# A held first store and two aligned loop heads in a masked softmax kernel

## The chip, the cores and the metric

The kernel runs on one core of one Trainium2 chip. The metric is the device time of one execution in microseconds (us); lower is better. The kernel before takes 156.9 us (median of four runs, 156.85 to 157.22). The granted clock was 1.0 in every run.

## The reference, cut to what matters

```python
batch, heads, seq_q, seq_k = 16, 8, 256, 256
x = randn(batch, heads, seq_q, seq_k)                  # float32, 33.6 MB
lengths = randint(seq_k // 2, seq_k, size=batch)       # one length for each batch entry
result = zeros_like(x)
for b in range(batch):
    n = lengths[b]
    e = exp(x[b, :, :, :n] - max(x[b, :, :, :n], axis=-1))
    result[b, :, :, :n] = e / sum(e, axis=-1)
```

Each batch entry is one *tile* of 2 MB: 128 partitions, 16 rows on each, 256 columns. The input is read once and the output written once. Columns beyond the length must come out as zero.

## The kernel before

Tiles 0 to 3 are loaded by SyncE, tiles 4 to 15 by GpSimd, which reads the tile's length and loads only about as many columns as are needed. VectorE masks a tile, ScalarE takes exponentials with row sums, VectorE divides, SyncE stores. There are eight tile slots in SBUF.

```python
# SyncE: five loads (tile 0 in halves), then all stores, on one queue
for h in range(2):
    nc.sync.dma_start(out=xt[:, 0, s], in_=x_f[0, :, s]).then_inc(s_ld[h], 16)
for b in range(1, ahead):                                    # ahead = 4
    nc.sync.dma_start(out=xt[:, b], in_=x_f[b]).then_inc(s_ld[b + 1], 16)
for b in range(batch):
    for s in parts(b):                                       # whole, halves or quarters of a tile
        nc.sync.wait_ge(s_out, ...)                          # VectorE has divided it
        nc.sync.dma_start(out=out_f[b, :, s, :], in_=xt[:, b % slots, s, :]).then_inc(...)
# GpSimd: waits, then a loop of 6 turns with two tiles each
nc.gpsimd.wait_ge(s_word, 16)                                # lengths are in SBUF
nc.gpsimd.wait_ge(s_fill, slots - ahead)                     # zeros are in slots 4 to 7
nc.gpsimd.wait_ge(s_ld[ahead - 1], 16)                       # tile 2 has landed
with nc.Fori(0, (batch - ahead) // 2, 1, engines=[POOL]) as q:
    for par in range(2):
        ...                                                  # read the length, wait for the slot
        pick(...)                                            # nested If/Else: one of 12 widths, one load
# ScalarE: a loop of 32 turns, half a tile each
with nc.Fori(0, 2 * batch, 1, engines=[ACT]) as i:
    nc.scalar.wait_ge(s_min, i + 1)
    ...                                                      # 8 activations, the last one increments s_exp
```

The softmax here doesn't subtract the row's maximum and nothing guards it: scores larger than these inputs give would overflow.

## Time and profile before

| What | Before | Where it is read |
|---|---|---|
| median of the runs | 156.9 us | timed runs |
| span of the profiled run | 155.3 us | page, first line |
| bytes moved, mean rate | 62.06 MB, 400 GB/s | page, HBM line |
| busiest engine | VectorE, 74% | page, busy totals |
| first store issued by SyncE | 18.86 us | timeline |
| first load issued by GpSimd | 20.94 us | timeline |
| instruction queue q14 | 2 packets | DMA queues |

The DMA engines limit this kernel: the DMA row is at 9 in 38 of 40 slices, and no compute engine is busier than 74%. So a profile of it is read by asking in which stretch the DMA engines move less than they can, not which compute engine is busy. The lines are in the prediction.

### The profile page before, as it was taken

The numbers are of one execution on the slowest core, as the hardware profiler recorded it, in microseconds if no ns is written. First come the engines' busy times: TensorE is split into PE (matmuls) and PEld (weight loads), VectorE is DVE, ScalarE is ACT, GpSimd is POOL, SyncE is SP. The second block draws the span as 40 slices with busy tenths as digits, with TensorE's granted clock in tenths as the row PEclk, the third lists the DMA queues.
The fourth block names the chain that finished last, engine by engine and source line by source line (L and its number), as shares of the span: only waits on it lengthen the run. The fifth ranks groups of instructions, "written<-read, shape, count | busy, mean of one in ns | idle before, by whom it ended". The sixth has DMA issues, their size and how long they took to land.

```text
span 155.3 us, 1316 instructions
## 1 busy us (share of the span) xinstructions
PE 0.2 (0%) x1; PEld 0.1 (0%) x1; DVE 115.6 (74%) x84; ACT 105.2 (68%) x514; POOL 19.0 (12%) x25
## 2 busy tenths in 40 slices
PE   0000000000000000000000000000000000000000
PEld 0000000000000000000000000000000000000000
DVE  1249999951999697997969696969698639796600
ACT  3087799992492978869595959596886906959100
POOL 4910031000220020200211020202000000000000
DMA  4999999999999999999999999999999999999991
GB/s 127 426 443 422 443 304 398 419 411 442 412 410 390 415 411 419 406 415 417 402 423 410 414 411 405 417 417 416 413 425 410 423 436 441 414 443 426 420 426 65
DMA packets 9988, 62.08 MB, mean 400 GB/s; under 512 B 850, under 2 KB 946, under 8 KB 6274
## 3 DMA queue, kind: packets, MB, share of 16 engines
q1 hardware_dynamic: 5904, 41.95, 65.7%
q0 software_dynamic: 4080, 20.12, 32.0%
q14 instruction: 2, 0.02, 0.0%
q10 hardware_dynamic: 2, 0.00, 0.0%
HBM read 28.51 MB, written 33.55 MB: 400 GB/s over the span
## 4 chain that ended last, share of the span: by engine, by line
DMA 77%; issue 7%; DVE 3%; ACT 3%; POOLq 3%; SPq 1%; ACTq 0%; POOL 0%; DVEq 0%
DMA xt<-in_x_dram 77%; ACT xt L252 3%; DVE xt L195 2%; DVE xt L222 1%; POOLq L99 1%; POOLq L135 1%; POOLq L130 1%; SPq L109 1%; ACTq L252 0%; POOL xt L130 0%; SPq L111 0%; POOLq L157 0%; DVE inv_sum L219 0%; POOLq L153 0%; POOLq L159 0%
## 5 line engine op out<-in xcount | busy, mean ns | idle before, releaser
L252 ACT ACTIVATE xt<-xt x256 | 102.4, 401 | 37.5 <-DVE xt L195 37.5
L222 DVE TENSOR_TENSOR xt<-xt,inv_sum 128x2048 f32<-128x2048 f32 x32 | 73.4, 2292 | 1.1
L252 ACT ACTIVATION_READ_ACCUMULATOR xt<-xt x256 | 47.8, 187 | 0.0
L195 DVE SCALAR_TENSOR_TENSOR xt<-down,len_s,xt 128x2048 f32<-128x2048 f32 (+1 forms) x17 | 37.8, 2222 | 13.3 <-DMA xt<-in_x_dram 13.2
L130 POOL DMA_DIRECT2D xt<-in_x_dram x12 | 12.8, 1064 | 95.6 <-issue 53.0
L219 DVE RECIPROCAL inv_sum<-row_sum 128x8 f32<-128x8 f32 x32 | 6.4, 199 | 14.4 <-ACT xt L252 14.4
L149 POOL MEMSET xt<- 128x1536 f32 x4 | 5.3, 1386 | 1.3 <-DVE len_s L186 1.3
L244 ACT ACT_TABLE_LOAD x1 | 1.3, 1283 | 1.6 <-SPq L79 1.6
L178 DVE TENSOR_SCALAR down<-iota_i 128x256 f32<-128x256 int32 x1 | 0.3, 298 | 1.6 <-POOL iota_i L141 1.6
L183 DVE CAST len_b<-word 1x16 bf16<-1x16 int32 x1 | 0.2, 161 | 0.5 <-DMA word<-in_lengths_dram 0.5
L186 DVE TENSOR_SCALAR len_s<-len_f 128x16 f32<-128x16 f32 x1 | 0.2, 175 | 0.4 <-PE len_f L165 0.4
L141 POOL IOTA iota_i<- 128x256 int32 x1 | 0.3, 332 | 0.6 <-SPq L79 0.6
L146 POOL MEMSET seed<- 1x1 f32 x2 | 0.3, 162 | 0.0
L244 ACT ACTIVATE warm<-const-float32-0.0 128x1 f32<-128x1 f32 x1 | 0.2, 203 | 0.0
L144 POOL MEMSET ones<- 1x128 bf16 x1 | 0.2, 194 | 0.0
L165 PE MATMUL len_f<-len_b,ones 1*128 1x16 bf16 x1 | 0.2, 168 | 2.8 <-DVE len_b L183 2.8
L270 POOL MEMSET const-float32-0.0<- 128x1 f32 x1 | 0.1, 98 | 0.3 <-issue 0.3
L165 PEld LDWEIGHTS len_f<-len_b,ones 1*128 1x128 bf16 x1 | 0.1, 97 | 2.7 <-POOL ones L144 2.7
L270 POOL MEMSET const-float32-1.0<- 128x1 f32 x1 | 0.1, 98 | 0.0
L270 POOL MEMSET const-bfloat16-1.0<- 128x1 bf16 x1 | 0.1, 98 | 0.0
L270 POOL MEMSET const-uint8-127<- 128x1 uint8 x1 | 0.1, 98 | 0.0
L270 POOL BASE_LOAD x1 | 0.0, 17 | 0.1
## 6 DMA issues: line engine op xcount, KB each, us to landing
out_dram<-xt SPq DMA_DIRECT2D x19, 1024.0 KB
out_dram<-xt SPq DMA_DIRECT2D x14, 512.0 KB
xt<-in_x_dram SPq DMA_DIRECT2D x3, 2048.0 KB, 16.2
out_dram<-xt SPq DMA_DIRECT2D x3, 2048.0 KB
xt<-in_x_dram POOLq DMA_DIRECT2D x3, 1728.0 KB, 17.0
xt<-in_x_dram POOLq DMA_DIRECT2D x2, 2048.0 KB, 18.9
xt<-in_x_dram POOLq DMA_DIRECT2D x2, 1600.0 KB, 17.2
xt<-in_x_dram POOLq DMA_DIRECT2D x2, 1280.0 KB, 14.5
```

The costliest lines, as they stand in the source:

```text
L99: return nc.values_load(at, engines=[engine], skip_runtime_bounds_check_because="compared with constants, never an address",)
L109: nc.sync.dma_start(out=xt[:, 0, s], in_=x_f[0, :, s]).then_inc(s_ld[h], 16)
L130: nc.gpsimd.dma_start(out=xt[:, slot, :, :w], in_=x_n[:, n, :, :w]).then_inc(s_sw[par], 16)
L135: with nc.gpsimd.If(v <= ws[m]):
L149: nc.gpsimd.memset(xt[:, b, :, low:], 0.0).then_inc(s_fill, 1)
L165: nc.tensor.matmul(len_f, lhsT=ones, rhs=len_b, start=True, stop=True).then_inc(s_lenf, 1)
L195: return nc.vector.scalar_tensor_tensor(out=t, in0=down[:, None, lo:hi].to_broadcast([P, s.stop - s.start, hi - lo]), scalar=len_s[:, b : ...
L219: step(nc.vector.reciprocal(out=inv_sum[:, b, s], in_=row_sum[:, b, s]))
L222: nc.vector.tensor_tensor(out=t, in0=t, in1=inv_sum[:, b, s, None].to_broadcast([P, half, seq_k]), op=ALU.mult,).then_inc(s_out, 1)
L244: nc.scalar.activation(out=warm, in_=nc.const_aps.tensor(0.0, (P, 1), F32), func=EXP)
L252: ins = nc.scalar.activation(out=e, in_=e, func=EXP, accum_out=sum_h[:, bass.ds(i, 1), j])
L270: nc = _bacc.Bacc("TRN2", target_bir_lowering=False, num_devices=1)
```

## The change

The intent, as far as the diff tells it: SyncE's first store is held a little, out of the way of the last loads, and the two loops that run from registers start at a fixed place of an instruction block. `head_slot` names that place; slot 0 is the head of the block.

```diff
         for b in range(1, ahead):
             nc.sync.dma_start(out=xt[:, b], in_=x_f[b]).then_inc(s_ld[b + 1], 16)
+
+        nc.sync.wait_ge(s_exp, 3)
         for b in range(batch):
...
-        with nc.Fori(0, (batch - ahead) // 2, 1, engines=[POOL]) as q:
+        with nc.Fori(0, (batch - ahead) // 2, 1, engines=[POOL], head_slot={POOL: 0}) as q:
...
-        with nc.Fori(0, 2 * batch, 1, engines=[ACT]) as i:
+        with nc.Fori(0, 2 * batch, 1, engines=[ACT], head_slot={ACT: 0}) as i:
```

## The prediction

> **What bounds the kernel now.** I read the page first: the busy totals, then the two DMA rows over 40 slices.
>
> ```profile
> PE 0.2 (0%) x1; PEld 0.1 (0%) x1; DVE 115.6 (74%) x84; ACT 105.2 (68%) x514; POOL 19.0 (12%) x25
> ...
> DMA  4999999999999999999999999999999999999991
> GB/s 127 426 443 422 443 304 398 419 411 442 412 410 390 415 411 419 406 415 417 402 423 410 414 411 405 417 417 416 413 425 410 423 436 441 414 443 426 420 426 65
> ...
> HBM read 28.51 MB, written 33.55 MB: 400 GB/s over the span
> ```
>
> No compute engine is above 74%, while the DMA row is at 9 in every slice but the first and the last. So the span is the time to move 62.06 MB plus the two ends at which nothing moves. One slice is 155.3/40 = 3.88 us. Only one inner slice stands out, the sixth (19.4 to 23.3 us): its engines are as busy as the others and yet it moves 304 GB/s.
>
> Second I cut the span into stretches. The columns are the stretch, its length, busy time of the five engines, the TensorE clock, the DMA share and GB/s.
>
> ```profile
> 5.00:20.30 15.30, 0.00 (x0) 0.00 (x0) 11.14 (x8) 10.15 (x51) 3.52 (x3) 1.00 1.02 434
> 20.30:23.30 3.00, 0.00 (x0) 0.00 (x0) 2.97 (x3) 3.00 (x16) 1.30 (x1) 1.00 0.99 284
> 23.30:36.00 12.70, 0.00 (x0) 0.00 (x0) 9.89 (x8) 12.61 (x64) 0.56 (x1) 1.00 0.99 409
> 36.00:134.00 98.00, 0.00 (x0) 0.00 (x0) 79.94 (x57) 69.45 (x343) 10.91 (x10) 1.00 1.02 416
> 134.00:152.00 18.00, 0.00 (x0) 0.00 (x0) 11.02 (x8) 8.49 (x42) 0.00 (x0) 1.00 1.00 425
> 152.00:155.30 3.30, 0.00 (x0) 0.00 (x0) 0.00 (x0) 0.00 (x0) 0.00 (x0) 1.00 0.07 27
> ```
>
> The reader sees 434 GB/s while only loads move, 409 to 416 with loads and stores together, 425 with stores alone, and in between a **dip** of 3.0 us at 284. The share in the dip is still 0.99, so the queues are not empty: the same packets take longer. Against 434 the dip loses 3.0 x (1 - 284/434) = 1.04 us. That is the only loss that this change can reach.
>
> Third, what happens in the dip, from the timeline (start, length) and, the last two lines, the chain of work that ended last:
>
> ```profile
> 18.86 0.42 SPq L118 DMA_DIRECT2D out_dram<-xt  x1
> 18.93 2.35 DVE L195 SCALAR_TENSOR_TENSOR xt<-down,len_s,xt 128x2048 f32<-128x2048 f32 x1
> ...
> 19.45 0.40 ACT L252 ACTIVATE xt<-xt  x1
> 19.76 0.19 ACT L252 ACTIVATION_READ_ACCUMULATOR xt<-xt  x1
> ...
> 20.94 1.30 POOL L130 DMA_DIRECT2D xt<-in_x_dram  x1 [12.42 <-issue]
> ```
>
> ```profile
> 20.95 0.50 POOL xt L130
> 21.48 1.37 POOLq L99
> ```
>
> SyncE issues its first store at 18.86 us, while the last of the five SyncE loads (tile 3) is still moving on the same queue: the DMA view of 20.3 to 23.3 us has 99.4% of its packets' time on q1, the SyncE queue, all but three of its packets full size. GpSimd begins its first own load at 20.94 us. Both stand ahead of the dip, so both are suspects.
>
> [...] Here the first load was issued at 1.13 us and the stretch 1 to 2 us moves nothing, so it is nearer 1.0 us; I use 1.0. [...] In this trace the instruction queue moved 2 packets in all, and the back edges of GpSimd's loop took 52 ns and of ScalarE's 45 ns (medians by source line), so no loop stalls now.
>
> **The change part by part.** *The wait.* It adds one condition to SyncE's first store; the instruction order confirms that only that store gains a semaphore, and no other instruction on SyncE moves. The third increment of that semaphore comes with ScalarE's 24th activation. The eight of tile 1's first half start at 16.64 and end with the accumulator read at 19.76 + 0.19 = 19.95 us. The store would so be issued at about 19.97 us instead of 18.86: 1.1 us later. Does that leave the DMA engines without work? Load 3 ends at 23.2 us at the dip's pace, or at 23.2 - 1.04 = 22.2 without a dip. The store can move from 19.97 + 1.0 = 21.0 us, at least 1.2 us earlier. So it costs nothing directly, and no DMA time is added.
>
> What it may save: if the queued store causes the dip, that begins 20.3 - 18.86 = 1.44 us after the issue, and would now begin at 19.97 + 1.44 = 21.4 us. From 20.3 to 23.3 us the engines did 3.0 - 1.04 = 1.96 us worth of full-rate work. At full rate until 21.4, 1.1 us of it is done, 0.86 us is left; at the dip's rate, 284/434 = 0.65, that takes 1.32 us and loses 0.46. Saving: 1.04 - 0.46 = about **0.6 us**. If the dip has another cause, the saving is zero.
>
> *The loop heads.* Each gets an alignment ahead of its loop: one jump executed once on each engine, some 0.05 us by the 52 ns of the branches here, plus at worst one block fetch. ScalarE reaches its loop at 3.1 us and its first data at 8.2: 5 us of slack hide that. GpSimd reaches its loop at 18.7 us, with nothing hidden there; I put a missed block at 1 to 2 us (an estimate, from the 1.0 us of a first byte here and 0.3 us for 8 KB at one engine's 434/16 GB/s). Its first load moves from 26.3 us on (the GpSimd queue, q0, has no packet in the DMA view before) and would then move at about 27.5. But store 0 alone fills the engines until about 28.3 us (2.1 MB at 409 GB/s after 23.2), with tile 1's stores queued behind it, so they would move stores meanwhile. In the loops nothing is removed, because there is no stall to remove. Cost on the path: zero.
>
> *Is a saving kept until the end?* Stores alone run from 134 us on at 425 GB/s with share 1.00, so the end is backlog, not the last tile's compute. The second-last tile's store is issued at 140.09 and can move at 141.1; but it and the last tile are 4.2 MB, 9.9 us at 425 GB/s, and end at 153.5, so it begins at about 143.6, behind the store ahead of it. So there is 2.5 us of slack, and 0.6 us carries to the end.
>
> Sum: 0 to -0.6 us from the wait, 0 from the loop heads.
>
> **The rivals.** (A) *The queued store slows the load ahead of it.* For: this is the only place where a load and a store share the SyncE queue and the only dip. GpSimd's second length read, at 21.48 us, takes 1.37 us against 0.50 for its first; later ones, beside stores, also take about 1 us[...]. Against: [...]the packets are not slower before 20.3. Result: 156.3 us.
>
> (B) *GpSimd's first transfer causes the dip*[...]. For: the strongest slowing, in the stretches of 21 to 23 us, starts with its DMA instruction at 20.94. Against: its third load, issued at 39.57, has one of 365 GB/s and then 467, so no dip as deep. Result: the dip stays, 156.9 us; if a block fetch delays GpSimd, the dip only moves along.
>
> (C) *The wait starves the engines or the alignment costs.* If load 3 ended by 21 us, or a fetch were far longer than I think, some tenths would be added: 157.2 us. Against: 1.2 us of margin in one case and 2.5 us of queued stores in the other.
>
> (D) *DVE or ScalarE becomes the bound.* Neither gets any work, and both have over a quarter of the span idle; I give it nothing.
>
> **Range and chances.** With 0.5 for A, 0.35 for B and 0.15 for C: 0.5 x 156.3 + 0.35 x 156.9 + 0.15 x 157.2 = 156.6. I lean a little to A, since someone chose that wait for a purpose: 156.5. The three runs before spread by 0.37 us. Range 155.9 to 157.1: A with a whole dip removed (156.89 - 1.04 = 155.85) at the bottom, C at the top. Two per cent is 3.1 us, three times all that the dip holds, so faster or slower by that much needs something not in this profile: 0.02 each.
>
> **What would show it.** The first store at about 20.0 us. Under A the dip starts about 21.4 us, load 3 ends near 22.7, and the sixth slice is well above 304 GB/s. Under B the dip keeps its place after GpSimd's DMA instruction. Loop heads: medians of the loops' branches unchanged; a gap of over 1 us between GpSimd's wait at 18.7 us and its length read would be a block fetch. The prediction is wrong if the time leaves the range, above all if the DMA row falls below 9 inside the span, or if the mixed rate of 416 GB/s changes with the order of the first transfers: each 1% of it over 98 us is 1 us, which I took to stay as it is.

The sum was 0 to -0.6 us: up to 0.6 us from the wait, 0 from the loop heads. The 1.0 us is measured: the first load was issued at 1.13 us and its first packet moved at 2.14.

## More of the kernel before

One more view of before is needed later, SyncE's own waits. Its columns are: who waited for whom, us in total, number of waits, longest wait.

```profile
SPq L117 <- DMA out_dram<-xt: 98.4, 14, 10.3
SPq L118 <- DVE xt L222: 26.9, 8, 15.0
```

SyncE mostly waits for older stores to land (98.4 us), that is, for DMA engines that are behind, and little for VectorE's results (26.9 us). So a finished store mostly lies ready before the DMA engines can take it.

## The result, and the profile after

The changed kernel takes **159.2 us** (median of four runs, 158.70 to 159.66) beside 156.91 for the kernel before. The ratio is **1.0141** (95% interval 1.0107 to 1.0176), 1.4% slower. Ratios here are the mean time of one kernel's runs over that of the other's in the same rounds, so not quite the ratio of the medians. It is well clear of noise and outside the predicted range of 155.9 to 157.1.

The page of the changed kernel, its DMA rows, and then two stretches of the prediction (stretch, length, busy time of five engines, clock, DMA share, GB/s):

```profile
DMA  4999999989999999999999999999999999996994
GB/s 110 436 430 432 432 422 420 412 241 415 436 436 303 375 413 418 408 422 408 408 418 408 421 406 417 412 413 417 418 416 416 421 422 434 420 451 266 403 399 199
...
q14 instruction: 6, 0.05, 0.1%
```

```profile
20.30:23.30 3.00, 0.00 (x0) 0.00 (x0) 2.97 (x3) 3.00 (x17) 0.00 (x0) 1.00 1.02 429
23.30:36.00 12.70, 0.00 (x0) 0.00 (x0) 10.50 (x8) 12.70 (x66) 1.86 (x2) 1.00 0.93 358
```

The dip at 20.3 to 23.3 us is gone: 429 GB/s instead of 284. But three other slices have fallen, to 241, 303 and 266 GB/s, and two of them have a DMA row below 9. Also, the instruction queue moved six packets instead of two. The timeline says what else is new (start, length):

```profile
20.56 7.82 SPq L120 DMA_DIRECT2D out_dram<-xt  x4
```

```profile
30.33 1.30 POOL L132 DMA_DIRECT2D xt<-in_x_dram  x1 [21.94 <-issue]
```

The first store comes at 20.56 us, about as predicted. GpSimd's first load comes at **30.33 us instead of 20.94**, 9.4 us later. Why is read by source line. Line 155 is GpSimd's loop statement and line 139 the Else branch of the nested choice. The columns are engine, operation, count, shortest/median/longest ns, and the first and last start in us.

```profile
L155 POOLq COMPARE_BRANCH  x7: 38/45/50, 19.5 to 121.3; - x7
L155 POOLq FUSED_REGOPS  x6: 78/78/95, 24.7 to 102.4; - x6
```

```profile
L139 POOLq COMPARE_BRANCH  x7: 38/38/38, 30.3 to 110.7; - x7
```

Before, the loop statement was line 153 and the Else branch line 137:

```profile
L153 POOLq FUSED_REGOPS  x6: 78/78/91, 18.9 to 98.2; - x6
```

```profile
L137 POOLq COMPARE_BRANCH  x7: 38/38/38, 20.9 to 105.9; - x7
```

There are seven branches instead of six: the new one is the jump to the loop head, at 19.5 us. The first instruction of the loop starts at 24.7 us, **5.2 us later**; before it started at once, at 18.9. Then the length is read, the width is chosen, the load's last register move is at 26.8 us, and the next instruction, the branch of line 139, is at 30.3: **3.5 us**, where the same pair took 0.7 us before (20.2 to 20.9). One q14 packet lies in each of these two gaps, 8192 bytes at 23.14 us and at 28.39 us, and each took 0.31 us. So in the changed kernel, GpSimd stood still twice for a piece of its own instructions.

SyncE's waits have turned over. Before, it waited mostly for DMA; now it waits mostly for VectorE:

```profile
SPq L120 <- DVE xt L224: 63.3, 21, 13.4
SPq L119 <- DMA out_dram<-xt: 51.3, 11, 7.2
SPq L117 <- DVE xt L224: 15.6, 1, 15.6
```

That is 78.9 us (63.3 + 15.6) instead of 26.9. The supply of finished stores has run out. The stretches with the losses, first before, then after:

```profile
31.00:36.00 5.00, 0.00 (x0) 0.00 (x0) 2.29 (x1) 4.91 (x26) 0.00 (x0) 1.00 1.01 410
36.00:47.00 11.00, 0.00 (x0) 0.00 (x0) 8.46 (x7) 5.96 (x30) 2.31 (x2) 1.00 1.01 422
47.00:53.00 6.00, 0.00 (x0) 0.00 (x0) 5.78 (x4) 2.91 (x16) 0.00 (x0) 1.00 1.03 403
53.00:142.00 89.00, 0.00 (x0) 0.00 (x0) 72.48 (x52) 66.69 (x331) 8.60 (x8) 1.00 1.02 418
142.00:146.00 4.00, 0.00 (x0) 0.00 (x0) 3.31 (x3) 2.37 (x12) 0.00 (x0) 1.00 1.00 430
```

```profile
31.00:36.00 5.00, 0.00 (x0) 0.00 (x0) 2.87 (x3) 5.00 (x27) 1.19 (x2) 1.00 0.85 276
36.00:47.00 11.00, 0.00 (x0) 0.00 (x0) 3.28 (x3) 1.20 (x6) 1.16 (x1) 1.00 1.03 428
47.00:53.00 6.00, 0.00 (x0) 0.00 (x0) 5.93 (x5) 5.78 (x30) 1.15 (x1) 1.00 0.99 320
53.00:142.00 89.00, 0.00 (x0) 0.00 (x0) 73.90 (x52) 64.94 (x320) 8.63 (x8) 1.00 1.02 418
142.00:146.00 4.00, 0.00 (x0) 0.00 (x0) 2.84 (x3) 3.31 (x17) 0.00 (x0) 1.00 0.61 258
```

Losses, each as length x (1 - rate after / rate before): 31 to 36 us 1.6 us, 47 to 53 us 1.2 us, 142 to 146 us 1.6 us. Gain: the dip at 20.3 us, 1.0 us, and a little at 36 to 47. The net is about 3.2 us, and the span grew by 2.4 (155.3 to 157.7). The remaining difference I did not take apart; part of it is the rounding of rates over long stretches.

How the lateness does this can be followed:
- *31 to 36 us.* The stores of tiles 0 and 1 are done, GpSimd's first load has only begun, and the share falls to 0.85: too little is queued.
- *36 to 47 us.* VectorE and ScalarE have nearly nothing to do (3.28 and 1.20 us busy), because tile 4 has not landed.
- *47 to 53 us.* So there is nothing to store, and GpSimd's loads run alone. From 49 to 51.5 us the DMA view has 102.6% of the packets' time on q0 and 297 GB/s; before, it was shared between both queues at 398.
- *142 to 146 us.* The last loads land late too, and the end of the kernel waits for compute of the last tiles instead of emptying a stock of stores. In the chain that ended last VectorE's share is 14%, after 3% before.

### The profile page after: what moved, and what is told of

It reads as the page before. It is cut to its first block, busy times and chain, and to the rows that moved or that the text cites. A ratio compares the mean times of both kernels' runs of the same rounds, so it can differ in the third digit from the quotient of the medians.

```text
span 157.7 us, 1319 instructions
## 1 busy us (share of the span) xinstructions
PE 0.2 (0%) x1; PEld 0.1 (0%) x1; DVE 115.6 (73%) x84; ACT 105.2 (67%) x514; POOL 19.0 (12%) x25
## 4 chain that ended last, share of the span: by engine, by line
DMA 68%; DVE 14%; issue 7%; ACT 4%; POOLq 1%; SPq 1%; ACTq 1%; DVEq 0%
DMA xt<-in_x_dram 62%; DVE xt L224 7%; DVE xt L197 6%; DMA out_dram<-xt 6%; ACT xt L254 4%; ACTq L254 1%; DVE inv_sum L221 1%; POOLq L137 1%; SPq L109 1%; POOLq L132 0%; SPq L111 0%; SPq L120 0%; DVEq L214 0%; POOLq L159 0%; POOLq L161 0%
```

## The experiments

My theory after the result: the jump to GpSimd's loop head costs everything, because its block fetches come while the DMA engines are full, and a late GpSimd starves the stores. The rivals: the held store starves the queues; ScalarE's head costs; the fetch traffic or the alignment itself costs, not the lateness. All kernels gave correct results. Diffs are against the kernel before unless said otherwise; each group of runs has its own runs of the kernel before on the same chip, with medians of 156.56 to 156.76 us. A "fetched block" below is one packet of the instruction queue (8192 bytes each in the changed kernel).

### The parts one by one

**The wait alone** (e1): both `head_slot` arguments removed from the changed kernel.

```diff
+        nc.sync.wait_ge(s_exp, 3)
```

> SyncE's wait alone, both loops as before. Theory (the jump to GpSimd's loop head costs all): no 5 us gap on GpSimd, first GpSimd load at about 21 us, time 156.3 to 157.1, so the wait alone is harmless. Rival (the wait starves the queues): 158 us or more. For the dip: if the queued store made it, it starts 1.1 us later and loses half as much; if GpSimd's first transfer made it, it stays at 20.3 to 23.3 us with about 284 GB/s.

Measured: 156.66 us, ratio 0.9983 (0.9961 to 1.0005). GpSimd's first load is at 20.79 us. In the dip:

```profile
20.30:23.30 3.00, 0.00 (x0) 0.00 (x0) 2.97 (x3) 3.00 (x17) 1.29 (x1) 1.00 0.99 360
```

360 GB/s instead of 284, with GpSimd where it was. The wait is not what costs. The dip follows the store and not GpSimd, as rival A of the prediction had it.

Repeated with five rounds (e15):

> The wait alone, repeated with more rounds. It halved the dip (0.5 us of DMA time). If that is kept until the end: 0.3 to 0.5 us faster, ratio 0.997 to 0.998. If it is lost again later: 0.999 to 1.001.

Measured: 156.24 us against 156.56, ratio 0.9981 (0.9964 to 0.9998). The wait alone is a small gain, 0.2%, just clear of zero. It is the only version here that beats the kernel before.

**Both heads, no wait** (e2), **GpSimd's head alone** (e3), **ScalarE's head alone** (e4): the `head_slot` arguments of the change, both or one at a time.

> Both loop heads aligned, no wait on SyncE. Theory: GpSimd stalls some 8 us as in the changed kernel, time 158.7 to 159.7. Rival (the wait is what costs): 156.9. If both are needed: in between, near 158.

> GpSimd's loop head alone. Theory: the whole loss, 158.5 to 159.5, perhaps some tenths less than with both, because ScalarE's two blocks are not fetched. Rival (ScalarE's head costs): 156.9.

> ScalarE's loop head alone. Theory: its jump stalls some 5 us from 1.8 us on but ends before its first data, so no ScalarE time is lost; [...]156.9 to 157.5. Rival: a good part of the 2.3 us.

| Kernel | Median us | Ratio (95% interval) | First GpSimd load |
|---|---|---|---|
| both heads | 159.85 | 1.0188 (1.0141 to 1.0234) | 30.54 us |
| GpSimd's head | 159.76 | 1.0210 (1.0177 to 1.0243) | 30.63 us |
| ScalarE's head | 156.88 | 1.0020 (0.9987 to 1.0052) | 21.42 us |

GpSimd's head is the loss. (The instruction queue moved six packets with both heads, four with either, two before.) Both kernels with it came out 0.15 to 0.3 us above the range that was expected. The dip at 20.3 us is there in the first two (300 and 281 GB/s), with GpSimd not starting before 30 us; that refutes rival B of the prediction, GpSimd's first transfer as its cause. ScalarE's jump stalls too, but in its slack. In the changed kernel its loop statement reads:

```profile
L249 ACTq COMPARE_BRANCH  x33: 33/45/50, 1.8 to 146.9; - x33
L249 ACTq FUSED_REGOPS  x32: 41/41/47, 6.9 to 144.1; - x32
```

It jumps at 1.8 us and goes on at 6.9, with one q14 packet in between (5.34 us), while its first data come at 7.8.

### Is it the lateness or the fetch?

**GpSimd held, with no loop head aligned** (three kernels, with 3, 5 and 6 for N), and **GpSimd started earlier**:

```diff
         nc.gpsimd.wait_ge(s_ld[ahead - 1], 16)
+        nc.gpsimd.wait_ge(s_exp, N)
```

```diff
-        nc.gpsimd.wait_ge(s_ld[ahead - 1], 16)
+        nc.gpsimd.wait_ge(s_ld[ahead - 2], 16)
```

> The kernel before, no alignment, GpSimd held ahead of its loop until ScalarE's fifth half tile (about 26.3 us), so its first load comes at about 28.5 us without any fetch. Theory (only the lateness counts, not the fetch): a part of the loss, 157.3 to 158.5. Rival (fetch traffic or cold instructions cost): 156.9.

> The same with the sixth half tile: first GpSimd load at about 31.7 us, a little later than the 30.5 us of the aligned kernels. Theory: the whole loss, 159 to 160.5, with stores running out about 32 us, slow stretches near 48 to 52 us and DMA engines idle near 144 us as in the aligned kernels. Rival: 156.9.

> The kernel before with GpSimd held ahead of its loop until ScalarE's third half tile (about 19.95 us), so that its first load comes at about 22.1 us, as in the kernels that reach the loops early. If 1.2 us of lateness makes the rest: 157.4 to 158. By the line through the other held kernels (0.22 us for each us): 156.9. If neither this nor e16 costs, the fetched blocks are left as the cause.

> The kernel before with GpSimd waiting for tile 1 instead of tile 2, so its first load is issued near 16 us instead of 21. If the time goes with GpSimd's start on both sides (0.22 us for each us, from the held kernels), 155.5 to 156.2. If the start before is already early enough to keep both kinds of transfer going: 156.4 to 157.2.

| First GpSimd load | Kernel | Median us | Ratio (95% interval) |
|---|---|---|---|
| 15.74 us | started earlier | 156.92 | 1.0007 (0.9978 to 1.0036) |
| 20.94 us | before | 156.6 to 156.8 | 1 |
| 22.18 us | held, N = 3 | 156.61 | 0.9991 (0.9960 to 1.0021) |
| 28.68 us | held, N = 5 | 158.32 | 1.0105 (1.0084 to 1.0127) |
| 32.17 us | held, N = 6 | 159.35 | 1.0177 (1.0160 to 1.0194) |

Lateness alone, with no loop head aligned, costs most of the loss. It is free up to at least 22.2 us, and from there to 32.2 us it costs about 0.3 us for each us (159.35 - 156.61 over 9.99 us is 0.27). Starting 5 us earlier gains nothing: my straight line through zero was wrong on that side. The kernel with N = 6 shows the same two late stretches as the changed kernel:

```profile
31.00:36.00 5.00, 0.00 (x0) 0.00 (x0) 2.24 (x1) 4.84 (x25) 1.85 (x2) 1.00 1.02 417
47.00:53.00 6.00, 0.00 (x0) 0.00 (x0) 5.93 (x5) 6.00 (x31) 1.15 (x1) 1.00 0.93 277
...
142.00:146.00 4.00, 0.00 (x0) 0.00 (x0) 2.84 (x3) 3.31 (x17) 0.00 (x0) 1.00 0.63 270
```

It lacks the loss at 31 to 36 us, and it keeps the dip at 20.3 us (273 GB/s). The kernel with both heads and no wait (e2) likewise has its dip and no such loss, 409 GB/s over 23.3 to 36 us, where the changed kernel has 358. So the wait on the store and the late GpSimd go badly together: by the stretches, the changed kernel lost more at 31 to 36 us (1.6 us) than the wait had gained at 20.3 (1.0 us). Whether anything of the gain reaches the end there isn't settled: 1.0141 and 1.0188 (e2) come from different groups of runs, and their intervals overlap.

### Why the fetch takes so long

**A fetch in the quiet** (e9, one look): ScalarE's head alone, with SyncE's first load held until ScalarE's warm-up has ended. Slower on purpose.

```diff
+        nc.sync.wait_ge(s_warm, 1)
         for h in range(2):
             s = slice(h * half, (h + 1) * half)
             nc.sync.dma_start(out=xt[:, 0, s], in_=x_f[0, :, s]).then_inc(s_ld[h], 16)
...
-        nc.scalar.activation(out=warm, ..., func=EXP)
+        nc.scalar.activation(out=warm, ..., func=EXP).then_inc(s_warm, 1)
```

> ScalarE's loop head aligned; SyncE's first load is held until ScalarE's warm-up activation ends (3.1 us instead of 1.1), so that the block is fetched while the DMA engines are idle. Slower by about 2 us on purpose. If the 5.1 us of the fetch are waiting behind bulk transfers: the gap from ScalarE's jump (1.8 us) to the next instruction of its loop is under 2.5 us. If a fetch takes 5 us by itself: again about 5 us.

```profile
L250 ACTq COMPARE_BRANCH  x33: 33/45/50, 1.8 to 142.6; - x33
L250 ACTq FUSED_REGOPS  x32: 41/41/47, 4.2 to 139.8; - x32
```

From the jump at 1.8 to the loop at 4.2 us: 2.4 us instead of 5.1. The single run took 158.7 us. So in this one look, on ScalarE, about half of the gap is there without the loads; the other 2.7 us come only beside them. I put those down to waiting for the DMA engines.

**Smaller transfers ahead of the fetch** (e10): GpSimd's head, with load 3 and store 0 issued in quarters. The cut shows the loads; tile 0's list of parts, VectorE's wait for load 3 and a wait of SyncE ahead of the stores were changed to match.

```diff
-            nc.sync.dma_start(out=xt[:, b], in_=x_f[b]).then_inc(s_ld[b + 1], 16)
+            for j in range(4 if b == 3 else 1):
+                s = slice(j * quarter, (j + 1) * quarter) if b == 3 else slice(0, nt)
+                nc.sync.dma_start(out=xt[:, b, s], in_=x_f[b, :, s]).then_inc(s_ld[b + 1], 16)
...
```

> GpSimd's loop head at slot 0 as in the run with that head alone, with load 3 and store 0 issued as four transfers of 512 KB each instead of one of 2 MB. If a fetch waits for the share of the one transfer that an engine is in the middle of[...]: the two gaps shrink from 6.3 and 3.4 us to about 1.5 to 3 us each, and the time lies near 157.5. If it waits for all that is queued: gaps and time as before, 159 to 160.

Measured: the jump is at 18.6 us and the loop at 24.1, still 5.5 us; 160.10 us, ratio 1.0235 (1.0197 to 1.0272). My idea that a fetch waits only for the one transfer in progress fell. It fits the other idea, that it waits for what is queued, but this run alone does not show how an engine chooses.

**Other slots of the block** (e8, e14): `head_slot={POOL: 64}` and `{POOL: 104}`, GpSimd only.

> The kernel before with GpSimd's loop aligned to slot 64 of a block instead of slot 0. [...] Theory (a fetch costs, an alignment does not): either no gap after the jump and 156.4 to 157.1, or a fetch with a gap of about 5 us and 158.5 to 160; gap and loss must go together. Rival (any alignment costs): a loss without a gap.

> GpSimd's loop aligned to slot 104, no other change. If the kernel's own position is between slots 64 and 104, the jump stays inside the block: no gap after the jump, and if an alignment as such is free, 156.4 to 157.1, provided that the rest of the loop is held too. If a gap of 5 us shows again, 158.5 to 160.5.

At slot 64 the jump at 18.8 us is followed by the loop at 25.4: a gap of 6.6 us, first load at 30.58 us, 160.41 us, ratio 1.0220 (1.0184 to 1.0256). At slot 104 the loop goes on at once (18.7 to 18.9 us), so the jump is free there. But the load's last register move at 20.5 us is followed by the next branch at 27.0, a gap of 6.5 us: first load at 27.05 us, 157.40 us, ratio 1.0073 (1.0030 to 1.0116). That is 0.3 us above the range expected for a jump without a gap, and it lies on the table of lateness above (about 1.008 between its rows). So not the alignment costs, but the gap. That a missing piece of instructions makes the gap is read from the packets of the changed kernel; for these two runs the packets are not shown.

### Moving the fetch out of the way

**The jump made early** (e5): in the changed kernel, GpSimd's three waits are moved from ahead of the loop into it.

```diff
-        nc.gpsimd.wait_ge(s_word, 16)
-        nc.gpsimd.wait_ge(s_fill, slots - ahead)
-        nc.gpsimd.wait_ge(s_ld[ahead - 1], 16)
         with nc.Fori(0, (batch - ahead) // 2, 1, engines=[POOL], head_slot={POOL: 0}) as q:
+            nc.gpsimd.wait_ge(s_word, 16)
+            nc.gpsimd.wait_ge(s_fill, slots - ahead)
+            nc.gpsimd.wait_ge(s_ld[ahead - 1], 16)
```

> The changed kernel, with GpSimd's three waits moved from ahead of its loop into the loop, so that the jump to the loop head is made at about 3 us and its block fetches run while GpSimd would wait anyway. Theory (the late fetches cost all): GpSimd's first load at about 21.5 us, time as with the wait alone, 156.4 to 157.3. Rival (the position of the loop in its block, or the extra waits, costs in each turn): 158.5 or more.

Measured: GpSimd's first load at 22.05 us, 157.55 us, ratio 1.0062 (1.0036 to 1.0088). More than half of the loss is gone, but not all. I then took parts away: SyncE's wait (e12), ScalarE's head (e13), and both heads, which leaves only the waits in the loop (e16).

> Both heads aligned and reached early, no wait on SyncE. If what remained (0.6%) came from the store being held to 21.1 us: the store at about 20 us, and 156.5 to 157.2. If it came from the four fetched blocks: about 157.5 as with the wait.

> GpSimd's head aligned and reached early, SyncE's wait kept, ScalarE's loop as before. Two blocks fewer during the first loads[...], the store is issued near 20.4 us. If the lateness of the store makes the rest: 156.7 to 157.3. If any fetched block of GpSimd costs: 157.5.

> The kernel before with GpSimd's three waits moved into its loop, no alignment. If the waits in each turn make the rest: 157.4 to 158. If not: 156.3 to 157.0.

| Kernel | Median us | Ratio (95% interval) | First GpSimd load | SyncE's 2 MB loads, issue to landing |
|---|---|---|---|---|
| heads early, wait | 157.55 | 1.0062 (1.0036 to 1.0088) | 22.05 us | 17.3 us |
| heads early, no wait | 158.00 | 1.0090 (1.0068 to 1.0111) | 22.09 us | 17.3 us |
| GpSimd's head early, wait | 157.87 | 1.0078 (1.0056 to 1.0100) | 21.89 us | 17.1 us |
| waits in the loop alone | 156.68 | 1.0002 (0.9966 to 1.0038) | 20.61 us | 15.9 us |

Taking away the wait, ScalarE's blocks or both heads was meant to find the remaining 0.6 to 0.9%. Only without GpSimd's head is it gone, and by the kernel held with N = 3 a start at 22 us alone does not make it. By exclusion GpSimd's blocks would be left, fetched during the first loads: with them those loads land more than 1 us later than in the last row (the landing is the median of three).

But the stretches do not show one common loss. First the kernel with heads early and the wait, then the one without the wait:

```profile
26.00:31.00 5.00, 0.00 (x0) 0.00 (x0) 4.97 (x4) 5.00 (x27) 0.00 (x0) 1.00 0.94 284
```

```profile
142.00:146.00 4.00, 0.00 (x0) 0.00 (x0) 2.82 (x3) 4.00 (x22) 0.00 (x0) 1.00 0.60 254
```

In both kernels with the wait (stores issued at 21.08 and 20.92 us) the loss lies at 26 to 31 us, 284 and 272 GB/s after 405 before. From 28 to 31 us alone the DMA shares are 0.88 and 0.81, after 0.97 before: the engines lack work there. Without the wait (20.01 us) that stretch moves 389, and the loss lies at 142 to 146 us instead, 254 GB/s after 430, as in the late kernels. So in the first and third rows a store held too long is not excluded, by itself or together with the blocks; the run below (e7), with no head at all, also loses 0.7% with its store at 21.53 us. What makes the 0.6 to 0.9% stays open: no run adds that traffic alone.

In the late kernels there is a remainder too: with a first load at 30.5 to 30.6 us the aligned ones without the wait lost 1.9 to 2.2%, while the table of lateness, read between 28.68 and 32.17 us, gives about 1.4%. The changed kernel itself, with 1.4% at 30.33 us, lies on the table.

**A store held longer** (e7): SyncE waits for VectorE's mask of tile 2 instead.

```diff
+        nc.sync.wait_ge(s_min, 6)
```

> No alignment; SyncE's first store waits for VectorE's mask of tile 2 (about 21.3 us) instead of ScalarE's third half tile (19.8). If the queued store slows the load ahead of it, the dip at 20.3 to 23.3 us is gone (over 420 GB/s, after 284 before and 360 with the shorter wait), and the time is 155.9 to 156.6. If the remaining 360 had another cause: still about 360. If the queue runs dry before the store comes: a share below 0.95 near 23 us and 157 or more.

Measured: the store is issued at 21.53 us and the dip is nearly gone, 412 GB/s. But the next stretch, 23.3 to 36 us, falls to 385 from 409, and the kernel is slower: 157.82 us, ratio 1.0066 (1.0041 to 1.0092). The loss was not removed, it moved. The share stays at 0.99, so the queue did not run dry either. Load 3 was issued at 3.5 us and landed 20.4 us later, before 24, so most of this stretch is without it. Why the first stores and GpSimd's first loads then take longer together I can't say; 12.7 x (1 - 385/409) is 0.75 us, most of the 1.16 us by which the medians differ.

## Why the prediction was wrong

**Right:** The DMA engines are the bound. The store was issued at 20.56 us (20.0 predicted, a little later because the loads landed later). The dip follows the queued store, rival A: with GpSimd unmoved it shrank as the store came later, 284, 360, 412 GB/s for stores at 18.86, 19.80 and 21.53 us, and in the changed kernel it is 429. (Each figure is one profile; in the other kernels with the store at 18.6 to 18.8 us and load 3 whole, and GpSimd not started earlier, it was 273 to 322.) The loop heads save nothing in the loops. ScalarE's stall is covered by its slack of 5 us, which was just enough.

**Right in kind, wrong in size:** 0.6 us was promised for the wait. Alone it is worth 0.3 us by the ratios of both groups. The dip lost 3.0 x (1 - 360/434) = 0.51 us instead of 1.04, as worked out, but part of that did not reach the end; and with a longer wait everything is given back.

**The step that failed** is the one on the cost of GpSimd's loop head: "I put a missed block at 1 to 2 us", "Its first load ... would then move at about 27.5", "Cost on the path: zero". Three things were wrong in it.
1. *The count.* One fetched piece of 8192 bytes was not enough for its loop. The jump and the first way out of the nested choice each waited, with one packet in each gap.
2. *The size.* The two waits took 5.2 and 3.5 us. I had made the estimate from an idle DMA path, and even there the measured fetch is 2.4 us. But the jump was made at 19.5 us, with the last 2 MB load still moving: q1's packets took 101.1% of the 16 engines' time from 19.4 to 24.8 us. I did not put the estimate beside the fact that this kernel's DMA row is at 9 in every slice but the first and the last.
3. *The cushion.* I argued that stores would fill the engines meanwhile. For the 1.2 us that I allowed it holds, and the run held with N = 3 confirms it: 1.2 us of lateness is free. For 9.4 us it doesn't. The stock of stores ends at about 32 us, tile 4 lands late, nothing can be stored around 47 to 53 us, and the last tiles' compute is exposed at 142 to 146 us.

The prediction had this as part of its rival C, "a fetch were far longer than I think", with 0.15 for C as a whole, and gave it some tenths of a us; it cost 2.3 us. Its signs of being wrong came as it had named them: the gap of over 1 us ahead of the length read, the DMA row below 9 inside the span, and the rate from 36 to 134 us at 411 instead of 416 GB/s. One reading was off without bearing on this: load 3 does not end at 23.2 us; in the kernel before it was issued at 3.3 us and took 21.8 us to land, until about 25.

The trace of before could not show the stall, because there GpSimd went into its loop without a gap (18.81 to 18.87 us) and the two q14 packets came later, at 26.5 and 60.4 us. It did show the premise: GpSimd stands at its waits until 18.7 us and reaches the loop only then.

**What stays open:** how a store behind a load in the same queue makes the dip; why the loss moves to GpSimd's first loads when the store is held longer; and what costs the 0.6 to 0.9% in the kernels with an early fetch.

## What to carry to other kernels

In this case a jump to a loop head was followed by a gap of 2.4 us ahead of the first loads (one look, on ScalarE) and of 5.1 to 6.6 us beside them, except at slot 104; a second gap, inside the loop, took 3.5 us, and 6.5 at slot 104. So don't force a jump to a new block on an engine that issues transfers, at a moment when the queues are full. Look at the instruction queue's packets and at gaps between a branch and the next instruction whenever code is moved or aligned. An engine that issues loads can start late at no cost and then at a cost: here the first 1.2 us were free and each later one cost about a quarter of a us, because the loss shows up elsewhere, where the other direction has run out of work.
